# A hybrid decoder trunk in float32 parts: low parts of projection weights by adding transfers, and convolution taps spread over the mixer stage

## The chip, the core and the metric

The kernel runs on one core of a Trainium2 chip. The core has TensorE (matmuls; PE in the profile), VectorE (DVE), ScalarE (ACT), GpSimd (POOL) and SyncE (SP), each with its own queue of instructions that it works through in order, and 16 DMA engines that they share. The metric is the time of one execution on the device in microseconds, as a median of several runs.

## The reference, cut to what matters

Two layers over a sequence of 1024 tokens with 1024 features, in float32. Each layer is a mixer and then a convolutional feed-forward network, both between two RMS norms. The mixer's input projection has 24 blocks of 128 columns, which feed four groups:

```python
proj = rms_norm(x, norm_mix_pre[l]) @ w_in[l]
(c_a, c_gate, sb_q, sb_k, sb_v, r_q, r_k, r_v, r_g, sc_b, sc_c, sc_h) = jnp.split(proj, 12, axis=-1)
y_conf = conformer_conv(c_a, c_gate, conf_dw_w[l], conf_dw_b[l], conf_ln_g[l], conf_ln_b[l])
y_sb = merge_heads(stick_breaking_attention(split_heads(sb_q), split_heads(sb_k), split_heads(sb_v)))
y_ret = retention_mixer(r_q, r_k, r_v, r_g, ret_norm_g[l])
y_sc = short_gated_conv(sc_b, sc_c, sc_h, sc_conv_w[l])
mix = jnp.concatenate([y_conf, y_sb, y_ret, y_sc], axis=-1) @ w_out[l]
...
def conformer_conv(a, gate, dw_w, dw_b, ln_g, ln_b):
    h = a * jax.nn.sigmoid(gate)
    h = causal_dwconv(h, dw_w) + dw_b     # 31 taps
    return jax.nn.silu(layer_norm(h, ln_g, ln_b))
```

Stick-breaking attention takes scores, a running sum along the keys of their softplus, an exponential, and a product with the values. Retention works in chunks of 128 tokens with a state carried from chunk to chunk.

## The kernel before, in words

**Number format.** A float32 matmul is made of three in a faster rounded format: every operand is split into a rounded high part and the rest, the low part, and high x high, high x low and low x high are added up in PSUM. For a block of projection weights (`load_weight`, lines 189 to 196) a transfer brings the 512 KB into `wr`, of which there is one buffer; ScalarE rounds it into `wh` (L193), and VectorE subtracts to get `wl` (L195). `wh` and `wl` have two buffers each, so the split of a block waits until the projection before the current one is done with its buffers.

**Slots.** The mixer's work is interleaved by hand. The 24 projections run in `IN_ORDER`; each has eight steps of six matmuls (L210), and after each step `run_slot` runs whatever has been entered for that slot: a slot is one such step, and 192 of them make the projections of a layer. The first two projections go together (`project_pair`, slots 0 to 15); projection n covers slots 8n to 8n + 7. What a projection gives is taken from PSUM by `evict`, and that enters later work: ten units of stick-breaking per pair of heads, scores at `SB_SLOT` + 6 k (L361 to L381: matmuls, three ScalarE passes, a VectorE step L375, scans on VectorE L379, an exponential), their transposes seven slots later and their products with the values ten slots later; retention from `RET_SLOT` on (state steps L474 to L479, scores L494 to L497, output L513 to L523, each output taken from PSUM by one ScalarE and two VectorE steps); the conformer's layer norm at `LN_SLOT`. The region's TensorE instructions keep the order in which they are traced. The order of the other engines is made by a scheduler from its own estimates of time and from priorities.

**The long convolution.** When the sigmoid gate of a conformer pair is done (kind "cg"), the convolution is entered in `conv`: a start on ScalarE (L268) and 30 taps on VectorE (L261), two times a layer. `run_slot` adds 0.8 to a credit in each slot, from the first slot on, and traces one step of the convolution for each whole credit, with a priority 1000 lower than other work.

**PSUM.** Projections alternate between banks 0 and 1. Stick-breaking's scores use bank 2, and retention takes bank 2 or the free one of the other two, by the slot (`bank`): bank 2 if the slot's number modulo 8 is not 0, 2 or 4.

**Tables.** ScalarE's sigmoid needs another function table than its exponential and logarithm; `ln_exp_tables` asks for the latter back.

Of the kernel before, what the change touches and what calls it, by code (L numbers as in the profile page):

```python
# [7 lines left out]
F32 = mybir.dt.float32  # L8
F32R = mybir.dt.float32r
AF = mybir.ActivationFunctionType  # L10
ALU = mybir.AluOpType
# [24 lines left out]


IN_ORDER = [
# [7 lines left out]
]  # L46
CONV_LATER = 1000
CONV_RATE = ((999, 0.8),)
REGION = 2
SB_SLOT = (20, 108)  # L50
SB_STEP = (6.0, 5.5)
SB_T = 7
SB_V = 10
RET_SLOT = 94, 160
RET_AT = (0, 6, 9, 12, 14, 17, 18, 23, 25), (0, 7, 9, 12, 14, 17, 18, 24, 26)
RET_PRE = 6, 3
LN_SLOT = 170
HOLD = 30
ROT_HOLD = 0
CONVH = 0  # L60
# [7 lines left out]
OTHER = (0, 2, 4)  # L68
HPR = 1000
HPW = 0  # L70
WPOOL = []
UPOOL = ()
SKEW = 0
NPLAIN = 3
# [12 lines left out]
def trunk_kernel(ctx, tc, x, w_in, w_out, w_up, w_down, params, gains, consts, rope, out):  # L87
    nc = tc.nc
# [25 lines left out]
    def ualloc(dt=F32, shape=(P, T)):  # L114
        s = free.pop(0)
        count[0] += 1
        t = big.tile(list(shape), dt, tag=f"u{s}", name=f"u{s}_{count[0]}")
        slot_of[id(t)] = (s, t)
        return t

    def ufree(*ts):
        for t in ts:
            free.append(slot_of.pop(id(t))[0])
# [15 lines left out]
    def ln_exp_tables():  # L139
        tc.keep_in_program_order(nc.scalar.preload_act_table_set("natural_log_exp_and_others"))  # L140
# [48 lines left out]
    def load_weight(src, eng):  # L189
        raw = wp.tile([P, KT, P], F32, tag="wr", name="wr", bufs=WR)  # L190
        nc.sync.dma_start(raw, src)
        wh = wp.tile([P, KT, P], F32R, tag="wh", name="wh")
        nc.scalar.copy(wh, raw)  # L193
        wl = wp.tile([P, KT, P], F32R, tag="wl", name="wl")
        eng.tensor_sub(wl, raw, wh.bitcast(F32))  # L195
        return wh, wl

    queue = []
# [351 lines left out]

    psum("pp")
    nc.scalar.preload_act_table_set("natural_log_exp_and_others")
    queue += [(w_in[0, n], nc.gpsimd if n in WPOOL else nc.vector) for n in range(24)]
    hhs = []
    for t in range(NB + SKEW):
        if t == XP:
# [22 lines left out]
    for l in range(DEPTH):  # L579
# [5 lines left out]
        def at(slot, fn, order=0):  # L585
            events.setdefault(slot, []).append((order, fn))

        conv = []
        credit = [0]
        slot = [0]  # L590

        def bank():

            s = slot[0]
            return (s // 8 + 1) % 2 if s < 192 and s % 8 in OTHER else 2

        def run_slot():
            for _, fn in sorted(events.pop(slot[0], ()), key=lambda e: e[0]):
                fn()
            credit[0] += next(r for end, r in CONV_RATE if slot[0] < end)  # L600
            while conv and credit[0] >= 1:
                credit[0] -= 1
                with tc.high_priority(offset=-CONV_LATER):
                    if next(conv[0], 0) == 0:
                        conv.pop(0)
            slot[0] += 1

        wo = []
# [15 lines left out]
        def evict(kind, i, ps, cs):  # L624
            if kind == "ca":
                st["a", i] = ualloc()
                nc.scalar.copy(st["a", i], ps)
            elif kind == "cg":
                s = ualloc()
                nc.scalar.activation(s, ps, AF.Sigmoid)  # L630
                if i == 1:
                    ln_exp_tables()
                nc.vector.tensor_mul(s, s, st["a", i])
                ufree(st["a", i])
                conv.append(conv_start(L, s, i, y, lambda h: at(slot[0] + HOLD, lambda: ufree(h))))
            elif kind == "sq":
                st["q"] = stick_q(ps)
                st["units"] = []
                for k in range(10):
                    u = dict(q=st["q"][k // 5], k=st["k"][k // 5], hh=k // 5, grp=SB_GROUPS[k % 5],  # L640
                             last=k % 5 == 4)
                    st["units"].append(u)
                    base = SB_SLOT[i] + int(SB_STEP[i] * k)
                    at(base, lambda u=u: stick_scores(u))
                    at(base + SB_T, lambda u=u: stick_transpose(u))
                    at(base + SB_V, lambda u=u: stick_values(u))
            elif kind == "sk":
                st["k"] = stick_k(ps)
            elif kind == "sv":
                ve = ualloc()  # L650
                nc.scalar.copy(ve, ps)
                v2 = []
                at(slot[0] + 2, lambda: v2.extend(value_tiles(ve)))
                y[2 + i] = ualloc()
                for u in st["units"]:
                    u.update(v=v2, y=y[2 + i])
            elif kind == "rk":
                st["rk"] = rotate(ps, cs, later)
            elif kind == "rq":
                st["rq"] = rotate(ps, cs, later)  # L660
            elif kind == "rv":
                rv = ualloc()
                nc.scalar.copy(rv, ps)
                k, kt2, q2, v2, gate = [], [], [], [], []
                rk, rq = st["rk"], st["rq"]
                st["gate"] = gate

                def keys():
                    h, lo = ualloc(F32R), ualloc(F32R)
                    split(h, lo, rk)  # L670
                    k.extend((h, lo))
                    kt2.extend(key_tiles(rk))

                def queries():
                    v2.extend(value_tiles(rv))
                    for half in range(2):
                        q2.append(ualloc(F32R, (P, 4, 2, P)))
                        split(q2[half][:, :, 0, :], q2[half][:, :, 1, :],
                              rq[:, half * 512:(half + 1) * 512].rearrange("p (c t) -> p c t", t=P))
                    ufree(rq)  # L680

                at(RET_SLOT[i] - RET_PRE[0], keys)
                at(RET_SLOT[i] - RET_PRE[1], queries)
                ret = retention(L, i, q2, k, kt2, v2, gate, y, bank)
                def ret_step(ret=ret):
                    with tc.high_priority(offset=HPR):
                        next(ret)

                for a in RET_AT[i]:
                    at(RET_SLOT[i] + a, ret_step)  # L690
            elif kind == "rg":
                gs = ualloc()
                nc.scalar.activation(gs, ps, AF.Silu)
                ln_exp_tables()
                st["gate"].append(gs)
            elif kind == "xh":
                st["h"] = ualloc()
                nc.scalar.copy(st["h"], ps)
            elif kind == "xc":
                nc.vector.tensor_mul(st["h"], st["h"], ps)  # L700
                acc = ualloc()
                w = L + C_SW + 3 * i
                nc.scalar.activation(acc, st["h"], AF.Copy, scale=par[:, w + 2:w + 3])
                for _ in conv_taps(acc, st["h"], w, 3):
                    pass
                ufree(st["h"])
                y[6 + i] = acc
            elif kind == "xb":
                nc.vector.tensor_mul(y[6 + i], y[6 + i], ps)

        sq = []
        at(LN_SLOT, lambda: layer_mean(y, sq))
        at(LN_SLOT + LN_VAR, lambda: layer_var(L, y, sq))
        cs = None
# [328 lines left out]
        with tc.manual_schedule(engines={mybir.EngineType.PE}):  # L1043
# [4 lines left out]
            for j in range(NPLAIN, NF):  # L1048
                end = j == NF - 1
# [14 lines left out]
        for ci, ch in enumerate(chunks):  # L1064
            final = ci == len(chunks) - 1
            if final:
                if not last:
                    queue += [(w_in[l + 1, n], nc.gpsimd if n in WPOOL else nc.vector) for n in range(24)]
                    prefetch(2)
                g_post, g_pre = gain(4 * l + 3), None if last else gain(4 * l + 4)  # L1070
            pairs = [loads[j] for j in ch]
            gs, ws = [p[0] for p in pairs], [p[1] for p in pairs]
            for t in range(NB):
                if final and last and t == NB - 1:
                    down_end(gs, ws, t)
                else:
                    down_tok(gs, ws, t, ci == 0, final)
                if t in (0, 1) and ci and todo and not final:
                    j, where = todo.pop(0)
                    loads[j] = down_load(j, where)  # L1080
            if places[ci] is None:
                for g, w in zip(gs, ws):
                    ufree(*g, *w)
            if ci == 0:
                for _ in range(4):
                    j, where = todo.pop(0)
                    loads[j] = down_load(j, where)
# [74 lines left out]
```

## Time and profile before

| | |
|---|---|
| median of three runs | 2382.75 us (2381.59 to 2386.46) |
| the profiled execution | 2386.67 us, of which 2384.9 is the span from the first to the last instruction |
| TensorE busy | 2297.3 us (96% of the span), 10596 matmuls; granted clock 0.986 |
| VectorE busy | 1674.2 us (70%) |
| ScalarE busy | 1080.7 us (45%) |
| GpSimd busy | 196.5 us (8%) |

Busy time of TensorE is the time in which at least one matmul is under way; the matmuls overlap, 390 ns each at a spacing of 228 ns. The granted clock is the share of full speed that the chip allowed TensorE. The mixer of layer 0 lies from about 20 to 580 us of the span, that of layer 1 from about 1210 to 1770, each with the output projection and the beginning of the feed-forward network behind it; the rest is the feed-forward network.

### The profile page before, as it was taken

The numbers are of one execution on the slowest core, as the hardware profiler recorded it, in microseconds if no ns is written. First come the engines' busy times: TensorE is split into PE (matmuls) and PEld (weight loads), VectorE is DVE, ScalarE is ACT, GpSimd is POOL, SyncE is SP. The second block draws the span as 40 slices with busy tenths as digits, with TensorE's granted clock in tenths as the row PEclk, the third lists the DMA queues.
The fourth block names the chain that finished last, engine by engine and source line by source line (L and its number), as shares of the span: only waits on it lengthen the run. The fifth ranks groups of instructions, "written<-read, shape, count | busy, mean of one in ns | idle before, by whom it ended". The sixth has DMA issues, their size and how long they took to land.

```text
span 2384.9 us, 26334 instructions
## 1 busy us (share of the span) xinstructions
PE 2297.3 (96%) x10596; PEld 1885.0 (79%) x10596; DVE 1674.2 (70%) x1749; ACT 1080.7 (45%) x1463; POOL 196.5 (8%) x84
## 2 busy tenths in 40 slices
PE   7998999999999999999999989999999999999998
PEld 6876787787888888788778767877888888888886
DVE  4699877559777777644556998775598777774445
ACT  5663565434455445421246535654344554453112
POOL 0000000000000000643210000000000000016420
PEclk9998999999999999999999989999999999999999
DMA  4212212412122224522222122123122222235223
GB/s 150 71 53 63 62 36 88 138 48 92 68 88 89 80 80 143 183 80 98 80 80 71 53 62 62 36 95 135 53 89 80 80 80 89 87 121 176 84 71 124
DMA packets 58810, 209.87 MB, mean 88 GB/s; under 512 B 7104, under 2 KB 7872, under 8 KB 58688
## 3 DMA queue, kind: packets, MB, share of 16 engines
q1 hardware_dynamic: 58688, 208.19, 26.7%
q8 instruction: 83, 1.36, 0.2%
q14 instruction: 39, 0.32, 0.0%
HBM read 159.93 MB, written 39.85 MB: 84 GB/s over the span
## 4 chain that ended last, share of the span: by engine, by line
PE 38%; DVE 7%; ACT 3%; DMA 1%; issue 1%; DVEq 0%; SPq 0%
PE pp L984 10%; PE pp L210 9%; PE ppx L901 8%; PE ppy L901 4%; DVE u L261 2%; PE ppz L901 2%; PE pp L738 1%; DVE u L182 1%; ACT u L151 1%; DMA wr<-in_w_out 1%; PE op L409 1%; DVE u L379 1%; DVE u L167 1%; PE tp L396 0%; DMA wr<-in_w_up 0%
## 5 line engine op out<-in xcount | busy, mean ns | idle before, releaser
L261 DVE SCALAR_TENSOR_TENSOR u<-u,par,u 128x1023 f32<-128x1023 f32 (+10 forms) x280 | 356.3, 1284 | 28.6 <-ACT u L793 24.4
L210 PE MATMUL pp<-hH,wh 128*128 128x512 f32 x960 | 327.2, 411 | 1.0 <-DVE u L182 0.5
L997 DVE TENSOR_TENSOR u<-u,pp 128x1024 f32<-128x1024 f32 x143 | 174.6, 1221 | 209.9 <-PE pp L984 209.8
L210 PE MATMUL pp<-hL,wh 128*128 128x512 f32 x960 | 312.7, 396 | 0.0
L210 PE MATMUL pp<-hH,wl 128*128 128x512 f32 x960 | 311.5, 395 | 0.0
L984 PE MATMUL pp<-u,u 128*128 128x512 f32 x1152 | 266.0, 392 | 6.1 <-ACT u L955 4.6
L984 PEld LDWEIGHTS pp<-u,u 128*128 128x128 f32 x1152 | 216.6, 189 | 52.4 <-ACT u L955 5.4
L974 POOL TENSOR_TENSOR hH<-u,hH 128x1024 fp32r<-128x1024 f32 x24 | 58.1, 2451 | 1946.5 <-ACT hH L973 1946.5
L210 PEld LDWEIGHTS pp<-hL,wh 128*128 128x128 f32 x960 | 183.6, 191 | 40.4
L210 PEld LDWEIGHTS pp<-hH,wl 128*128 128x128 f32 x960 | 183.2, 191 | 40.3
L210 PEld LDWEIGHTS pp<-hH,wh 128*128 128x128 f32 x960 | 172.6, 193 | 37.5 <-issue 5.9
L738 PE MATMUL pp<-u,hH 128*128 128x512 f32 x512 | 140.2, 392 | 0.4 <-ACT u L181 0.4
L984 PE MATMUL pp<-hH 128*128 128x512 f32 x576 | 131.5, 389 | 0.0
L984 PEld LDWEIGHTS pp<-hH 128*128 128x128 f32 x576 | 108.1, 188 | 22.4
L901 PE MATMUL ppx<-u,wh 128*128 128x512 f32 x384 | 118.4, 389 | 0.3 <-ACT u L926 0.3
L793 ACT ACTIVATE u<-u,par 128x1024 f32<-128x1024 f32 x76 | 87.8, 1156 | 67.4 <-DVE u L947 65.6
L738 PEld LDWEIGHTS pp<-u,hH 128*128 128x128 f32 x512 | 95.0, 188 | 20.4 <-ACT u L181 1.2
L195 DVE TENSOR_TENSOR wl<-wr,wh 128x1024 fp32r<-128x1024 f32 x60 | 73.3, 1221 | 50.9 <-ACT wh L193 50.7
L973 ACT CAST u<-u 128x1024 fp32r<-128x1024 f32 x48 | 50.2, 1052 | 128.9 <-DMA u<-in_w_down 85.7
L901 PE MATMUL ppx<-u,hH 128*128 128x512 f32 x352 | 108.4, 389 | 0.0
L193 ACT CAST wh<-wr 128x1024 fp32r<-128x1024 f32 x60 | 63.0, 1051 | 71.3 <-PE pp L210 57.1
L379 DVE TENSOR_TENSOR_SCAN u<-pp,u 128x1023 f32<-128x1023 f32 (+3 forms) x64 | 87.8, 1403 | 0.7
(240 smaller groups left out, 4400.3 us busy)
## 6 DMA issues: line engine op xcount, KB each, us to landing
wr<-in_w_up SPq DMA_DIRECT2D x50, 512.0 KB, 3.5
wr<-in_w_in SPq DMA_DIRECT2D x48, 512.0 KB, 3.5
gd<-u SPq DMA_DIRECT2D x44, 512.0 KB, 2.9
u<-in_w_down SPq DMA_DIRECT2D x44, 512.0 KB, 4.3
u<-gd SPq DMA_DIRECT2D x44, 512.0 KB, 3.9
u<-in_w_up SPq DMA_DIRECT2D x38, 512.0 KB, 4.3
xs<-u SPq DMA_DIRECT2D x24, 512.0 KB, 2.6
u<-xs SPq DMA_DIRECT2D x24, 512.0 KB, 3.4
```

The costliest lines, as they stand in the source:

```text
L193: nc.scalar.copy(wh, raw)
L195: eng.tensor_sub(wl, raw, wh.bitcast(F32))
L210: nc.tensor.matmul(ps[:, half * 512:(half + 1) * 512], w[:, kt, :], m[:, 4 * half:4 * half + 4, kt, :], start=(kt == 0 and m is hH and w i ...
L261: eng.scalar_tensor_tensor(acc[:, lo:hi], src[:, lo - s:hi - s], wc, acc[:, lo:hi], ALU.mult, ALU.add)
L379: nc.vector.tensor_tensor_scan(rev, z[:, o + 1:e + 1][:, ::-1], rev, r[:, e:e + 1], ALU.add, ALU.add)
L738: nc.tensor.matmul(ps[:, hs], a[:, t, k, :], w[:, hs], start=(k == 0 and a is hH and w is wo[k][0]), stop=(k == KT - 1 and a is hL))
L793: nc.scalar.activation(acc, ps, AF.Copy, scale=par[:, w + 2:w + 3])
L901: nc.tensor.matmul(ps, a[:, kt, :], x(m, kt), start=start and kt == 0 and a is wh and m == 0, stop=kt == 3 and a is wl, skip_group_check=True)
L973: nc.scalar.copy(h, raw)
L974: (nc.gpsimd if len(loads) >= 4 else nc.vector).tensor_sub(lo, raw, h.bitcast(F32))
L984: nc.tensor.matmul(ps[:, hs], a[:, ts_], w[:, hs], start=(i == 0 and w is h and a is gh), stop=(i == len(gs) - 1 and a is gl))
L997: nc.vector.tensor_add(facc[t], facc[t], ps)
```

## The change

Four things change together.

- The first conformer pair is projected first: columns "ca" 0 and "cg" 0 are the pair of slots 0 to 15, and stick-breaking's first keys, queries and values follow in slots 16 to 39. Its units start at slot 36 instead of 20. The exponential's tables are asked for after each of the two gates, which are no longer next to each other. The layer norm moves from slot 170 to 176.
- The steps of the convolution get 0.75 credit a slot up to slot 36 and 0.42 after; credit is held at 2 at most, and is 0 while no convolution is entered.
- Each tap is queued on VectorE behind the last instruction other than a tap that had been traced for VectorE three slots back (`CONV_LAG`). This is an order within VectorE's queue, not a wait for another engine.
- For projections from the third on (22 of 24 in a layer) the low part is made without VectorE: ScalarE writes the raw weights times -1 in the rounded format into `wl`, and a transfer issued by GpSimd adds the raw weights from HBM to it.

```diff
 IN_ORDER = [
-    ("sk", 0, 6), ("sq", 0, 4), ("sv", 0, 8),
-    ("ca", 0, 0), ("ca", 1, 1), ("cg", 0, 2), ("cg", 1, 3),
+    ("ca", 0, 0), ("cg", 0, 2), ("sk", 0, 6), ("sq", 0, 4), ("sv", 0, 8),
+    ("ca", 1, 1), ("cg", 1, 3),
...
-CONV_RATE = ((999, 0.8),)
+CONV_RATE = ((36, 0.75), (999, 0.42))
+CONV_LAG = 3
-SB_SLOT = (20, 108)
+SB_SLOT = (36, 108)
-LN_SLOT = 170
+LN_SLOT = 176
...
-        eng.tensor_sub(wl, raw, wh.bitcast(F32))
+        if eng is not None:
+            eng.tensor_sub(wl, raw, wh.bitcast(F32))
+            return wh, wl
+
+        nc.scalar.activation(wl, raw, AF.Copy, scale=-1.0)
+        nc.gpsimd.dma_start(wl, src, accum_op=ALU.add)
         return wh, wl
...
-    queue += [(w_in[0, n], nc.gpsimd if n in WPOOL else nc.vector) for n in range(24)]
+    queue += [(w_in[0, n], None if n >= 2 else nc.vector) for n in range(24)]
...
+        seen = [None]
+        marks = []
+
+        def mark_slot():
+
+            traced = nc.cur_bb.bb.instructions
+            mark = marks[-1] if marks else None
+            for i in reversed(traced):
+                if i is seen[0]:
+                    break
+                if i.engine == mybir.EngineType.DVE and i.name not in taps:
+                    mark = i
+                    break
+            seen[0] = traced[-1]
+            marks.append(mark)
+
+        taps = set()
+
         def run_slot():
             for _, fn in sorted(events.pop(slot[0], ()), key=lambda e: e[0]):
                 fn()
-            credit[0] += next(r for end, r in CONV_RATE if slot[0] < end)
+            mark_slot()
+            credit[0] = min(credit[0] + next(r for end, r in CONV_RATE if slot[0] < end), 2) if conv else 0
             while conv and credit[0] >= 1:
                 credit[0] -= 1
-                with tc.high_priority(offset=-CONV_LATER):
+                mark = marks[max(0, len(marks) - 1 - CONV_LAG)]
+                with ExitStack() as late:
+                    late.enter_context(tc.high_priority(offset=-CONV_LATER))
+                    if mark is not None:
+                        late.enter_context(tc.issue_after(mark))
+                    traced = nc.cur_bb.bb.instructions
+                    n = len(traced)
                     if next(conv[0], 0) == 0:
                         conv.pop(0)
+                    taps.update(i.name for i in traced[n:])
             slot[0] += 1
...
             elif kind == "cg":
                 s = ualloc()
                 nc.scalar.activation(s, ps, AF.Sigmoid)
-                if i == 1:
-                    ln_exp_tables()
+                ln_exp_tables()
```

The same choice of `None` for blocks from the third on stands where layer 1's weights are entered.

## Rows read from the trace of the kernel before

**Rows 1.** Busy time by stretch (us); x counts instructions, PEclk is the granted clock.

```profile
48.00:420.00 372.00, 351.02 (x1761) 285.52 (x1760) 298.53 (x349) 210.40 (x270) 0.00 (x0) 0.97 0.22 66
60.00:120.00 60.00, 60.00 (x312) 50.79 (x311) 39.76 (x44) 39.34 (x50) 0.00 (x0) 1.00 0.22 71
120.00:280.00 160.00, 139.94 (x687) 113.03 (x687) 152.49 (x171) 77.24 (x101) 0.00 (x0) 0.94 0.21 60
1300.00:1460.00 160.00, 141.56 (x677) 114.07 (x676) 151.86 (x167) 76.87 (x99) 0.00 (x0) 0.91 0.20 57
```

The columns of these rows: the stretch, its length, then busy us and instructions of PE, PEld, DVE, ACT and POOL, the granted clock, the DMA engines' busy share, GB/s.

**Rows 2.** The same view in slices of 20 us, layer 0.

```profile
160.00:180.00 20.00, 18.40 (x94) 15.33 (x93) 19.75 (x23) 8.26 (x14) 0.00 (x0) 1.00 0.16 53
180.00:200.00 20.00, 19.12 (x103) 15.96 (x102) 19.87 (x22) 6.91 (x8) 0.00 (x0) 1.00 0.09 27
...
220.00:240.00 20.00, 13.25 (x44) 9.96 (x43) 19.05 (x20) 4.92 (x7) 0.00 (x0) 0.74 0.22 77
240.00:260.00 20.00, 15.71 (x69) 12.67 (x68) 16.78 (x16) 8.78 (x12) 0.00 (x0) 0.83 0.26 79
...
280.00:300.00 20.00, 20.00 (x105) 16.74 (x104) 16.84 (x20) 12.35 (x17) 0.00 (x0) 1.00 0.19 53
...
340.00:360.00 20.00, 19.89 (x117) 16.96 (x116) 18.08 (x29) 10.79 (x19) 0.00 (x0) 1.00 0.07 27
```

**Rows 3.** The same view of line L210 alone: PE, PEld, clock, DMA.

```profile
48.00:120.00 72.00, 59.74 (x246) 44.58 (x245) 1.00 0.26 83
120.00:280.00 160.00, 104.39 (x406) 77.23 (x405) 0.94 0.21 60
```

**Rows 4.** VectorE's groups by line, 120 to 280 us.

```profile
L261 DVE SCALAR_TENSOR_TENSOR u<-u,par,u 128x1019 f32<-128x1019 f32 (+29 forms) x56 | 69.2, 1263 | 0.5
L379 DVE TENSOR_TENSOR_SCAN u<-pp,u 128x1023 f32<-128x1023 f32 (+7 forms) x13 | 18.2, 1433 | 0.1
L182 DVE TENSOR_TENSOR u<-tp,u 128x512 fp32r<-128x512 f32 x19 | 12.3, 683 | 0.0
L195 DVE TENSOR_TENSOR wl<-wr,wh 128x1024 fp32r<-128x1024 f32 x9 | 11.0, 1220 | 2.0 <-ACT wh L193 2.0
L375 DVE SCALAR_TENSOR_TENSOR u<-pp,u 128x1024 f32<-128x1024 f32 (+1 forms) x7 | 8.0, 1141 | 1.1 <-ACT u L373 1.1
```

The columns: line, engine, operation, tiles and shapes, count | busy us, mean ns of one | idle us before, and what ended it.

**Rows 5.** Timeline of VectorE: start us, us, instruction, count.

```profile
231.15 0.69 DVE L522 TENSOR_TENSOR u<-pp,u 64x512 f32<-64x512 f32 x1
231.77 1.25 DVE L261 SCALAR_TENSOR_TENSOR u<-u,par,u 128x1007 f32<-128x1007 f32 x1
233.05 0.68 DVE L523 TENSOR_TENSOR u<-pp,u 64x512 f32<-64x512 f32 x1
```

**Rows 6.** TensorE's waits, whole span: us in total, times, longest.

```profile
PE pp L513 <- DVE u L379: 8.6, 2, 4.3
...
PE pp L361 <- DVE u L379: 7.3, 6, 1.7
```

**Rows 7.** ScalarE's groups by line, 20 to 420 us.

```profile
L193 ACT CAST wh<-wr 128x1024 fp32r<-128x1024 f32 x23 | 24.2, 1051 | 22.7 <-PE pp L210 21.3 <-DMA wr<-in_w_in 1.4
...
L630 ACT ACT_TABLE_LOAD x2 | 2.6, 1283 | 0.0
```

**Rows 8.** Timeline of ScalarE at the end of the first pair, layer 0.

```profile
42.90 1.06 ACT L193 CAST wh<-wr 128x1024 fp32r<-128x1024 f32 x1 [9.12 <-PE pp L210]
...
48.57 1.02 ACT L328 ACTIVATE u<-pp 64x1024 fp32r<-64x1024 f32 x1 [1.18 <-PE pp L210]
```

**Rows 9.** The chain that ended last, in order of time: start us, us, what.

```profile
1222.60 9.13 PE pp L210 x40
```

**Rows 10.** DMA issues of the page: KB each, median us to landing.

```profile
wr<-in_w_in SPq DMA_DIRECT2D x48, 512.0 KB, 3.5
gd<-u SPq DMA_DIRECT2D x44, 512.0 KB, 2.9
...
u<-gd SPq DMA_DIRECT2D x44, 512.0 KB, 3.9
```

More of the change, by code (lines that the diff above doesn't have):

```diff
@@ L70 @@
 HPW = 0
-WPOOL = []
 UPOOL = ()
@@ L1067, in trunk_kernel @@
                 if not last:
-                    queue += [(w_in[l + 1, n], nc.gpsimd if n in WPOOL else nc.vector) for n in range(24)]
+                    queue += [(w_in[l + 1, n], None if n >= 2 else nc.vector) for n in range(24)]
                     prefetch(2)
```

## The prediction

> **What bounds the kernel now.** I read the page's busy times first (the table above): TensorE is busy 96% of the span, so only time in which TensorE waits, or runs at its lower clock, can be won back. Then the windows of the two mixer stages [rows 1]. From 60 to 120 us TensorE is busy all the time, with VectorE at 40 of 60 us. From 120 to 280 us in layer 0, and from 1300 to 1460 us in layer 1, VectorE is at 152 of 160 us, and TensorE is idle 20.1 and 18.4 us. The granted clock falls there to 0.94 and 0.91 (a mix of the levels 2.4 and 1.2 GHz): busy time times the missing share is 8.4 and 12.7 us. Together that is 59.6 us. A second reading counts matmuls: 312 in 60 undisturbed us make 5.2 per us, so the 687 and 677 matmuls need 132.1 and 130.2 us, and 28 and 30 us of each 160 are lost. The two readings agree: **58 us** are there to be won. In slices of 20 us [rows 2] the reader sees how it is lost. With VectorE full and the clock still at 1.00 TensorE loses 1.6 and 0.9 us a slice; at 220 to 260 us it loses 6.8 and 4.3 us and the clock falls to 0.74 and 0.83. With VectorE at 16.8 or 18.1 of 20 us, and hardly a tap, it loses 0.0 and 0.1 us.
>
> What fills VectorE there? Grouped by line, 56 taps of the long convolution (L261) take 69.2 us of the 160 [rows 4]. The timeline of VectorE [rows 5] shows the harm: between each two steps of retention's output (L522, L523) stands one or a pair of taps, so a chain that TensorE waits for gets 1.25 us longer at every link. TensorE's waits name L379, the scan of stick-breaking, whose score bank the next matmuls want [rows 6].
>
> **The change part by part.**
>
> *Taps.* Before, credit grows by 0.8 a slot from the first slot on, with no convolution yet there to use it, so more than thirty taps are traced at once at slot 47, with the lowest priority, and the rest soon after. Slots are counted in groups of six matmuls of L210: 246 of them stand from 48 to 120 us and 406 from 120 to 280 [rows 3], which is slots 16 to 56 and 56 to 123. After, the first convolution starts at slot 15: 21 slots at 0.75 give 15 steps, then 0.42 a slot, and the 64 steps end near slot 151. In slots 56 to 123 that leaves 68 x 0.42 = 28.6 taps for 56: 27.4 fewer, at 69.2 / 56 = 1.24 us each, makes -34 us of VectorE.
>
> *Low parts.* For 22 projections of a layer VectorE's subtraction (1.22 us, L195) becomes a second ScalarE pass (as L193, 1.05 us) [rows 4, 7] and an adding transfer from GpSimd's queue. In the same slots 9 x 1.22 = -11 us. ScalarE gains 22 x 1.05 = 23 us, and two table loads of 1.28 us a layer for the sigmoid that now stands alone [rows 7]: 26 us more on 210 of 372 us [rows 1]; it is covered. If ScalarE lacked the room, the 26 us would fall on the stick-breaking chain, which is a rival below.
>
> *Stick-breaking 16 slots later.* The first ten units move from slots 20 to 74 to slots 36 to 90, the second ten stay. Slots 56 to 123 then hold nine scored units instead of seven. One costs VectorE 1.14 (L375) + 18.2 / 7 = 2.6 (L379) + about two splits of 0.68 [rows 4], with the small additions of L417 and L418 some 6 us by my estimate: +12 us.
>
> So VectorE's load there goes from 152 to 152 - 34 - 11 + 12 = 119 us. TensorE's own work there is 160 - 29 = 131 us and some 8 us more for the two units (my estimate from 12 us between units less projections). 119 of 139 is 86%, inside the slices of [rows 2] that lose 0.0 to 0.1 us. But taps still stand in the queue, so I take a quarter of the mean of 1.6 and 0.9 us: 0.3 to 0.4 us a slice over slots 16 to 151, some 257 us (72 for slots 16 to 56, 131 to 123, and 28 more at the same 1.9 us): **5 us a layer**. The bounds are 1 us (the loaded slices without taps) and 16 us (the full ones).
>
> *The first late transfer.* The weight after the first pair cannot be split before the pair's first half ends: its copy starts at 42.90 us, and the pair ends at 48.57 [rows 8]. TensorE reads a low part after four matmuls, 4 x 9.13 / 40 = 0.9 us later [rows 9], so at 49.5. The new chain: two ScalarE passes, to 45.0 us, then the adding transfer. The trace has none. From below it is a plain load of the same 512 KB, 3.5 us; from above load, store and load again, 3.5 + 2.9 + 3.9 = 10.3 us [rows 10]. That is a stall of 0 to 5.8 us. I take one read of the weight and one pass over the destination, 3.5 + 2.9 = 6.4 us, since an addition must read both: landing at 51.4, **1.9 us a layer**. The Trainium skill, DMA: Bandwidth & Descriptors, section Anatomy of one DMA, gives 2.0 us plus bytes over 436 GB/s for a transfer of GpSimd's, an estimate of 3.2 us without the addition; by it this term would be 0, and the sum 3.8 us better for two layers. No run here shows it yet.
>
> *The later transfers.* The buffers of the projection before come free when a projection starts, and the next needs its low part 48 x 0.228 + 0.9 = 11.8 us later if nothing stands between its matmuls, and 257 / 17 + 0.9 = 16.0 us later on average over those 17 projections. The chain is 2.1 + 6.4 = 8.5 us: hidden. At 10.3 us it is 12.4, and the few bare projections lose 0.6 us each. Behind the waiting transfer on GpSimd's queue stands only the next one: GpSimd is idle in the stage [rows 1]. On SP's queue the next load waits for the raw weight's buffer, and the rotary copies and key copies queue behind it; that buffer is now free after ScalarE's second pass instead of after VectorE's subtraction, so they can only come sooner. The transfers add 44 reads of 512 KB to engines that are busy 0.22 of the stage.
>
> *A new wait.* The last unit of the first stick-breaking, scored at slot 90, uses the score bank that retention's first matmuls want at slot 94. The same pair three slots apart costs 4.3 us before (L513 waiting for L379) [rows 6]; four slots apart gives one slot, 6 x 0.228 = 1.4 us, more, and VectorE is less full. Bounds 0 and 4.3; I take **1.5 us a layer**.
>
> *The layer norm six slots later* (176, its second part 181) still ends ahead of the output projection at slot 192, with some 11 slots in hand: nothing.
>
> **Sum.** 58 us, less 2 x (5 + 1.9 + 1.5) = 17, makes 41 won. The profiled execution took 2386.7 us (span 2384.9 and 1.8 around it): 2345.7. It stood 3.9 us above the median of the three runs, so against the median I say **2342 us**.
>
> **The rivals.**
>
> *TensorE goes on waiting for the chains.* The taps are not the only length in a chain: ScalarE's passes and the scans stay, and the convolution now also runs in slots 120 to 151, where VectorE had room. For it: L361's waits for L379 are 1.7 us at the longest, about one tap [rows 6], so waits of that size survive wherever one tap is left. Against it: the loaded slices without loss. If the loss falls to 16 us a layer, the full slices' rate, the gain is 58 - 2 x (16 + 3) = 20 us: 2363.
>
> *The adding transfers arrive late (slower).* If a transfer takes D us, a projection waits when 2.1 + D passes 16.0 us on average; the 41 us are eaten when 44 transfers are each 0.9 us late, which is D of about 14.8, more than four plain loads. At D of 17 us the loss is 44 x 3.1 = 136 us: near 2478. A way to it: GpSimd makes the transfer's descriptors itself, and VectorE's instructions, back to back in this stage, keep it from doing so. The Trainium skill, SBUF — State Buffer, section Who interferes with whom, says that VectorE blocks GpSimd's descriptor writing in its two-port modes, and that tensor_tensor has none; the VectorE groups here are tensor_tensor, scans and scalar_tensor_tensor, so by it the blocking should not come, and no run here shows it. Against the rival: 10.3 us is already the sum of three plain transfers.
>
> *The stall only moves.* TensorE's order is fixed by hand; what is not lost to retention's chain is lost to the score bank at slot 94 at 4.3 us and to ScalarE's 26 us more a layer, where stick-breaking and the lone sigmoid meet. Then 2380, no difference.
>
> **How the numbers follow.** Forecast 0.63 (its own range 2324 to 2355), chains still waiting 0.18, late transfers 0.12, moved stall 0.07. By the count of matmuls at the best rate shown without loss that has the same mix, 105 in 20 us [rows 2], 58 us hold; with nothing left over the time would be 2325, and the idle time also hides restarts that the rows don't show, so the range begins at 2318. It ends at 2376, above the second case; beyond it lie the late transfers and the moved stall. A change under 0.2%, 4.8 us, can't be told from none here. Faster: 0.63 + 0.18 = 0.81; same 0.07; slower 0.12.
>
> **What would show it.** In the changed kernel's profile VectorE should be near 86% in slots 56 to 123, in place of 95%, and the granted clock should stay near 1.00 where it was 0.74. No subtraction L195 for projections after the second; GpSimd's transfers land 5 to 8 us after they are issued. TensorE should wait some 2 us for the low part at the first projection after the pair, and nowhere else for a low part. L513's wait for L379 should stand near the first retention step. I would be wrong if TensorE waits for low parts throughout (late transfers), or if VectorE is relieved and TensorE idles as before.

## The result, and the profile after

The changed kernel is slower: 2402.49 us median of four runs (2398.64 to 2405.79) against 2384.61 for the kernel before, a ratio of 1.0075 with a 95% interval of 1.0054 to 1.0097. 41 us were to be won and 18 were lost. The profiled execution took 2398.64 us, its span is 2396.9, 12.0 longer than before: the execution profiled before was the longest of its kernel's runs, this one is the shortest of its own. In what follows ratios are always to runs of the kernel before on the same chip; 1% is 24 us. Line numbers behind `load_weight` are 5 higher than before, behind `run_slot` 30 higher.

Busy time by stretch, three of the stretches of [rows 1]:

```profile
48.00:420.00 372.00, 350.48 (x1758) 285.24 (x1757) 273.09 (x325) 226.47 (x289) 18.17 (x21) 0.97 0.40 94
...
120.00:280.00 160.00, 143.53 (x728) 117.29 (x727) 118.60 (x146) 94.21 (x125) 7.79 (x9) 0.95 0.39 89
1300.00:1460.00 160.00, 143.96 (x738) 118.26 (x737) 119.29 (x146) 94.20 (x125) 7.76 (x9) 0.96 0.39 92
```

VectorE's load from 120 to 280 us fell from 152.5 to 118.6 us; I had worked out 119. And yet TensorE is busy 143.5 us there, little more than the 139.9 before, with the granted clock at 0.95. VectorE is no longer full, and TensorE still waits: it idles 16.5 of the 160 us, nearly as much as before (20.1), which is one of the two signs that the prediction named for being wrong. The slices of the same view (as [rows 2], and two of the output projection) show where:

```profile
160.00:180.00 20.00, 20.00 (x108) 16.88 (x107) 17.29 (x20) 15.91 (x21) 0.86 (x1) 1.00 0.25 53
180.00:200.00 20.00, 13.14 (x63) 10.69 (x62) 12.07 (x17) 11.32 (x17) 0.86 (x1) 0.83 0.24 53
220.00:240.00 20.00, 17.09 (x94) 13.07 (x92) 14.57 (x16) 10.04 (x13) 0.86 (x1) 1.00 0.40 105
240.00:260.00 20.00, 17.23 (x70) 14.29 (x71) 11.38 (x13) 9.59 (x13) 0.86 (x1) 0.74 0.39 106
...
420.00:440.00 20.00, 16.19 (x68) 11.93 (x66) 10.60 (x10) 4.55 (x5) 0.00 (x0) 1.00 0.41 131
440.00:460.00 20.00, 18.00 (x67) 14.66 (x68) 5.74 (x5) 4.02 (x4) 0.00 (x0) 0.83 0.27 79
```

The slices that [rows 2] show at 160 and 220 us are better, 20.0 for 18.4 and 17.1 for 13.3 us. The one at 180 us is bad now, 13.1 for 19.1 us, with VectorE at 12 of 20. And two slices of the output projection hold 68 and 67 matmuls where there were 87 and 84 (TensorE was busy 19.8 and 18.1 us there before, at a clock of 1.00).

Counted by TensorE's instructions in the two traces (six matmuls of L215, before L210, are a slot), the 24 projections of a layer take 396.4 and 396.7 us (layers 0 and 1) in place of 396.6 and 399.8, and the output projection behind them 105.6 and 103.7 in place of 97.4 and 95.9. Inside the projections something was won and lost again: in layer 0, slots 104 to 112 take 22.7 us for 32.6, and slots 88 to 96 take 28.2 for 16.3. TensorE's waits over the whole span (us in total, times, longest) put names to them:

```profile
PE tp L455 <- DVE u L182: 12.9, 4, 5.8
PE pp L768 <- ACT u L181: 10.3, 6, 3.7
PE pp L366 <- DVE u L384: 8.4, 4, 2.4
PE pp L215 <- DMA wl<-in_w_in: 6.4, 3, 3.5
...
PE pp L518 <- DVE u L384: 5.7, 2, 2.9
```

L518's wait for L384, which is L513 and L379 in [rows 6], fell from 8.6 to 5.7 us; all waits of retention's output (L518) together fell from 21.0 to 11.3. The first, second and fourth rows stand for what was added: retention's key transposes (L455) waited 1.1 us before, the output projection (L768) 0.4, and the low part of the first projection after a pair not at all. The third (L366, stick-breaking's scores) stood at 7.3 before.

**The first place, slot 88.** TensorE, ScalarE and VectorE, by their timelines (start us, us, instruction, idle before and what ended it):

```profile
179.62 1.11 PE L414 MATMUL op<-u,u 128*128 128x256 f32 x8
180.57 0.60 PE L455 MATMUL tp<-ident,u 128*128 128x128 f32 x4
187.00 1.11 PE L455 MATMUL tp<-ident,u 128*128 128x128 f32 x4 [5.83 <-DVE u L182]
```

```profile
179.08 1.28 ACT L723 ACT_TABLE_LOAD   x1
180.37 1.02 ACT L723 ACTIVATE u<-pp 128x1024 f32<-128x1024 f32 x1
181.41 1.28 ACT L140 ACT_TABLE_LOAD   x1
183.22 1.06 ACT L386 ACTIVATE u<-u 128x1024 f32<-128x1024 f32 x1 [0.52 <-DVE u L384]
184.18 1.04 ACT L199 ACTIVATE wl<-wr 128x1024 fp32r<-128x1024 f32 x1
185.25 0.36 ACT L421 COPY u<-op 64x256 f32<-64x256 f32 x1
185.64 0.59 ACT L181 CAST u<-tp 128x512 fp32r<-128x512 f32 x1
```

```profile
186.25 0.69 DVE L182 TENSOR_TENSOR u<-tp,u 128x512 fp32r<-128x512 f32 x1 [0.18 <-ACT u L181]
186.98 0.42 DVE L423 TENSOR_TENSOR u<-op,u 64x256 f32<-64x256 f32 x1
```

The product with the values (L414), the key transposes and the layer norm share two PSUM tiles. At slot 88 the values of stick-breaking's eighth unit (slot 36 + 42 + 10) take one and the first four transposes the other. The next four start when the first four have been split into high and low part (L181, then L182), so they wait for that tile; the values' tile is read until later still (L423). L181 stands in ScalarE's queue behind the retention gate with its two table loads, an exponential, the new second pass (L199) and the values' own readout (L421). The first four transposes are done at 181.2 us, and L181 starts 4.5 us after. Before, the last values of these units stood at slot 84.

**The second place, the output weights.** They too come through the one raw buffer, block by block. ScalarE's timeline, and SyncE's, which issues the loads, with VectorE's half of the split between them:

```profile
404.85 2.37 ACT L306 ACTIVATE u<-u,par 128x1024 f32<-128x1024 f32 x2
...
414.78 2.93 ACT L181 CAST hH<-u 128x1024 fp32r<-128x1024 f32 x3
417.61 1.05 ACT L181 CAST u<-wr 128x1024 fp32r<-128x1024 f32 x1
418.56 3.90 ACT L181 CAST hH<-u 128x1024 fp32r<-128x1024 f32 x4
427.90 1.05 ACT L181 CAST u<-wr 128x1024 fp32r<-128x1024 f32 x1 [5.44 <-DMA wr<-in_w_out]
```

```profile
422.39 1.22 DVE L182 TENSOR_TENSOR u<-wr,u 128x1024 fp32r<-128x1024 f32 x1
```

```profile
402.95 0.33 SPq L644 DMA_DIRECT2D wr<-in_w_out  x1
415.63 7.20 SPq L249 DMA_DIRECT2D u<-in_x  x2
423.63 0.33 SPq L644 DMA_DIRECT2D wr<-in_w_out  x1
```

ScalarE does not split the block issued at 402.95 before 417.61, since the layer norm's passes (the last is L306) and the splits of the mixed heads (L181 into hH) stand ahead of it. VectorE follows at 422.39, behind its own half of those splits, and only then is the buffer free. So the next load starts 20.7 us after this one, and TensorE waits for the last blocks one by one.

**The third place, the first low part** after the pair of layer 0:

```profile
42.62 1.05 ACT L193 CAST wh<-wr 128x1024 fp32r<-128x1024 f32 x1 [9.12 <-PE pp L215]
43.57 1.06 ACT L199 ACTIVATE wl<-wr 128x1024 fp32r<-128x1024 f32 x1
```

```profile
48.54 0.61 PE L215 MATMUL pp<-hL,wh 128*128 128x512 f32 x2
51.58 0.87 PE L215 MATMUL pp<-hH,wl 128*128 128x512 f32 x2 [2.43 <-DMA wl<-in_w_in]
52.25 1.05 PE L215 MATMUL pp<-hH,wh 128*128 128x512 f32 x2
```

```profile
wl<-in_w_in POOLq DMA_DIRECT2D x44, 512.0 KB, 7.4
```

The wait is 2.4 us here and 3.5 in layer 1; behind it pairs of matmuls take 1.05 us instead of 0.61, at the lower clock; the last row is the page's DMA issue, the median from issue to landing in us.

### The profile page after: what moved, and what is told of

Its sections match the earlier page's. It is cut to its first block, busy times and chain, and to the rows that moved or that the text cites. A ratio compares the mean times of both kernels' runs of the same rounds, so it can differ in the third digit from the quotient of the medians.

```text
span 2396.9 us, 26404 instructions
## 1 busy us (share of the span) xinstructions
PE 2297.6 (96%) x10596; PEld 1883.5 (79%) x10596; DVE 1626.8 (68%) x1705; ACT 1114.0 (46%) x1505; POOL 234.7 (10%) x128
## 3 DMA queue, kind: packets, MB, share of 16 engines
q8 instruction: 83, 1.36, 0.2%
## 4 chain that ended last, share of the span: by engine, by line
PE 35%; DVE 7%; ACT 5%; DMA 2%; issue 1%; DVEq 0%; SPq 0%; ACTq 0%
PE pp L1014 10%; PE ppx L931 8%; PE pp L215 6%; PE ppy L931 4%; PE pp L768 2%; PE ppz L931 2%; DVE u L266 1%; DVE u L384 1%; DVE u L182 1%; DMA wr<-in_w_out 1%; DMA wl<-in_w_in 1%; ACT u L181 1%; DVE u L380 1%; ACT u L377 0%; ACT u L151 0%
## 5 line engine op out<-in xcount | busy, mean ns | idle before, releaser
L266 DVE SCALAR_TENSOR_TENSOR u<-u,par,u 128x1023 f32<-128x1023 f32 (+6 forms) x280 | 359.1, 1283 | 40.8 <-ACT u L823 24.4
L215 PE MATMUL pp<-hH,wh 128*128 128x512 f32 x960 | 325.7, 410 | 0.4 <-ACT hH L181 0.4
L215 PE MATMUL pp<-hH,wl 128*128 128x512 f32 x960 | 311.7, 395 | 6.4 <-DMA wl<-in_w_in 6.4
L215 PE MATMUL pp<-hL,wh 128*128 128x512 f32 x960 | 312.0, 396 | 0.0
L215 PEld LDWEIGHTS pp<-hH,wl 128*128 128x128 f32 x960 | 182.6, 191 | 47.8 <-DMA wl<-in_w_in 8.1
L215 PEld LDWEIGHTS pp<-hL,wh 128*128 128x128 f32 x960 | 183.0, 191 | 40.2
L215 PEld LDWEIGHTS pp<-hH,wh 128*128 128x128 f32 x960 | 172.6, 192 | 36.3 <-issue 5.5
L1004 POOL TENSOR_TENSOR hH<-u,hH 128x1024 fp32r<-128x1024 f32 x24 | 58.2, 2452 | 1208.6 <-ACT hH L1003 1208.6
L768 PE MATMUL pp<-u,hH 128*128 128x512 f32 x512 | 145.6, 402 | 10.8 <-ACT u L181 10.3
L768 PEld LDWEIGHTS pp<-u,hH 128*128 128x128 f32 x512 | 96.9, 192 | 34.4 <-ACT u L181 12.8
L200 POOL DMA_DIRECT2D wl<-in_w_in x44 | 38.2, 868 | 710.9 <-ACT wl L199 588.3
L182 DVE TENSOR_TENSOR u<-tp,u 128x512 fp32r<-128x512 f32 x96 | 62.8, 685 | 44.1 <-ACT u L181 43.8
```

The lines of the kernel that those rows point to most:

```text
L182: nc.vector.tensor_sub(l, src, h.bitcast(F32))
L200: nc.gpsimd.dma_start(wl, src, accum_op=ALU.add)
L215: nc.tensor.matmul(ps[:, half * 512:(half + 1) * 512], w[:, kt, :], m[:, 4 * half:4 * half + 4, kt, :], start=(kt == 0 and m is hH and w i ...
L266: eng.scalar_tensor_tensor(acc[:, lo:hi], src[:, lo - s:hi - s], wc, acc[:, lo:hi], ALU.mult, ALU.add)
L768: nc.tensor.matmul(ps[:, hs], a[:, t, k, :], w[:, hs], start=(k == 0 and a is hH and w is wo[k][0]), stop=(k == KT - 1 and a is hL))
L1004: (nc.gpsimd if len(loads) >= 4 else nc.vector).tensor_sub(lo, raw, h.bitcast(F32))
```

## The experiments

The first four were to tell two theories apart: that the stalls had only moved (A), or that the adding transfers cost the time (B). "The mended kernel" is that of the fifth experiment.

**Low parts on VectorE again.**

```diff
-    queue += [(w_in[0, n], None if n >= 2 else nc.vector) for n in range(24)]
+    queue += [(w_in[0, n], nc.vector) for n in range(24)]
```

The same is done for layer 1.

> The changed kernel with the low parts of all 24 projections made by VectorE's subtraction again; order of projections, taps and slots stay as changed. Theory A (the stalls moved: stick-breaking's tail meets retention's start near slot 88, and the later layer norm delays the output weights): the wait for the first adding transfer goes, 4 us a layer, and VectorE gets 27 us a layer more work, so 2390 to 2410 us against 2402, and the 5.8 us wait of the key transposes (L455) and the waits of the output projection for ScalarE stay. Theory B (the adding transfers are what costs, by ScalarE's second pass and by traffic): the loss goes, 2375 to 2386 us, and those two waits go too.

Measured 0.9985 (0.9973 to 0.9998): 0.9%, 21 us, are back. On the time B is right and A wrong. On the places it is the other way round for one of the two: the key transposes wait nearly as long as in the changed kernel (5.4 us at the longest for 5.8), and the output projection waits a third as long.

```profile
PE tp L455 <- DVE u L182: 10.8, 2, 5.4
...
PE pp L768 <- ACT u L181: 3.5, 3, 2.3
```

**Layer norm at slot 170.**

```diff
-LN_SLOT = 176
+LN_SLOT = 170
```

> The changed kernel with the layer norm at slot 170 as before. Theory A: the split of the fourth block of output weights no longer stands behind the layer norm on ScalarE; the output projection's waits for ScalarE (10.3 us in the span, 7 to 8 us a layer with the slower clock behind them) go, and the time falls by 12 to 15 us, to 2387 to 2391. Theory B: the output weights are late because of ScalarE's extra passes and of the transfers, not the norm's slot; within 4 us of 2402.

Measured 1.0018 (1.0005 to 1.0030), 14 us back; L768 waits 0.2 us in the span instead of 10.3. As A said.

**Stick-breaking's first units closer.**

```diff
-SB_STEP = (6.0, 5.5)
+SB_STEP = (5.5, 5.5)
```

> The changed kernel with stick-breaking's first ten units 5.5 slots apart instead of 6, so that its last values come at slot 95 instead of 100 and none stand at slot 88, where retention's keys are transposed. Theory A: the excess of the projection at slots 88 to 95, 10 us a layer, falls to 4 or less, and the time by 8 to 14 us, to 2388 to 2394. Theory B: no collision at that slot, so the wait only moves to another place; within 4 us of 2402.

Measured 1.0019 (1.0007 to 1.0031), 13 us back; L455's wait falls from 12.9 to 3.0 us. As A said. The edit moves nine of the ten units, though, so it is not shown that all of the 13 us are this one meeting's.

**The adding transfers alone, on the kernel before.** The edit is that of `load_weight` and of the two `queue` lines.

> The kernel before with the adding transfers alone; order, taps and slots as before. Theory A: two costs of about 2 to 4 us for the first transfer of a layer, and 11 us less VectorE work a layer in the stretch where VectorE is full, which TensorE gets back at half to full rate: 2365 to 2382 us against 2385. Theory B: 2395 to 2405, with TensorE waiting for low parts or for what ScalarE does late.

Measured 1.0083 (1.0066 to 1.0099), 20 us lost: B again, and against my sum, by which VectorE's relief should have paid for the first transfers. TensorE waits for two low parts, 8.5 us in all, and slots 16 to 24, where they fall, take 19.3 and 18.8 us in this trace for 12.1 before: some 14 of the 20 us. So neither theory was enough. Theory C took both: the taps win, and three costs eat it.

**Three undone together.** Low parts on VectorE, norm at 170, step 5.5.

> The changed kernel with three things undone or mended together: low parts by VectorE, layer norm at slot 170, stick-breaking's first units 5.5 slots apart. Theory C, formed after the first four runs: the spread taps do win some 18 us a layer, and three separate costs eat it, each with its place: the adding transfers (first projection after the pair, output weights), stick-breaking's tail against retention's start, the late norm. Then the three add up but for what two of them share in the output projection (7 us): 2402 - 21 - 15 - 15 + 7 = 2358, between 2352 and 2366. Rival D: the three are one shortage seen at three places, and mending one mends most: 2372 to 2384.

Measured 0.9916 (0.9902 to 0.9930), 2364.16 us: **20 us faster than the kernel before**, and 38 us faster than the changed one. Singly the three gave back 0.90, 0.57 and 0.56%, 2.03% or 48 us; 10 of those are shared, 3 more than the 7 I took for the output projection. C holds; the rival D (one shortage at three places) would have been at 2372 or more.

**Low parts on GpSimd.**

```diff
-    queue += [(w_in[0, n], None if n >= 2 else nc.vector) for n in range(24)]
+    queue += [(w_in[0, n], nc.gpsimd if n >= 2 else nc.vector) for n in range(24)]
```

> The changed kernel with the low parts of the third and later projections subtracted by GpSimd (2.4 us as its other subtractions take) in place of ScalarE's second pass and the adding transfer; VectorE is as free as with the change. Theory C: the loss of the transfers goes, since the chain to the first low part is 1.05 + 2.4 us instead of 2.1 + 7, and ScalarE has 23 us a layer less: 2378 to 2388. Rival: GpSimd's reads and VectorE's hold each other up, VectorE's taps get longer than 1.27 us, and it stays above 2392.

Measured 1.0032 (1.0020 to 1.0045), 2390 us, between the two expectations: 10 of the 21 us come back. The rival's mechanism is there; how much of the other 11 us it makes is not shown. Of VectorE's groups, 120 to 280 us, this is the first:

```profile
L266 DVE SCALAR_TENSOR_TENSOR u<-u,par,u 128x1000 f32<-128x1000 f32 (+24 forms) x25 | 34.0, 1360 | 0.3
```

With the low parts on VectorE 25 taps take 31.6 us, 1264 ns each. The median is 1.27 us in both, so a few taps are held up: the longest takes 2.8 us in this stretch (3.3 between 48 and 420 us), against 1.28.

**The third projection's low part on VectorE too.** `None if n >= 3`.

> The changed kernel with the third projection's low part also by VectorE, so that the first adding transfer of a layer is that of the fourth. Theory C: the wait at the first projection after the pair (excess 4.3 and 3.8 us) goes, the rest of the transfers' cost, in the output projection, stays: 2392 to 2396. Rival: the wait moves to the next projection, which has no other TensorE work between its steps either: 2398 to 2403.

Measured 1.0063 (1.0048 to 1.0079): 3 us back, which the intervals do not tell from none, 2399 us, as the rival said. TensorE's wait for low parts is 6.4 us in all as in the changed kernel, in three waits: in layer 0 it moved to the next projection. Starting the transfers one weight later does not help.

**The taps alone, on the kernel before.** Old order and slots, low parts on VectorE, 0.55 credit a slot, held at 2, queued three slots back.

```diff
-CONV_RATE = ((999, 0.8),)
+CONV_RATE = ((999, 0.55),)
+CONV_LAG = 3
```

> The kernel before with nothing changed but the taps: 0.55 credit a slot (the 64 steps end near slot 163), credit held at 2, queued three slots back; old order, old slots, low parts by VectorE. If spreading the taps is what wins: the excess of 17 us a layer at slots 104 to 111 falls below 9, and the time to 2350 to 2368. If the earlier start is needed, since the taps now fill slots 120 to 163 as well: 2376 or more.

Measured 0.9950 (0.9934 to 0.9966), 2371 us, between the two expectations: 12 us won by the taps alone, without the earlier start.

**The same slots and credit without the queueing.** The mended kernel of the fifth experiment.

```diff
-                    if mark is not None:
-                        late.enter_context(tc.issue_after(mark))
```

> The mended kernel (low parts by VectorE, norm at 170, step 5.5; 2364 us) with the taps at the same slots and the same credit, but not queued behind VectorE's work of three slots back. If the spread credit alone wins: 2360 to 2368. If the queueing does part of it, taps go ahead of chain steps again and the excess of slots 88 to 119 grows: 2372 or more.

Measured 1.0000 (0.9989 to 1.0010): the queueing is worth 0.84%, 20 us, all that the mended kernel had won over the kernel before. Taps in the stretch of slots 88 to 103 (stretch, length, VectorE's busy us and count, clock, DMA), first without and then with the queueing:

```profile
184.00:223.00 39.00, 20.14 (x17) 0.96 0.21 55
```

```profile
177.00:211.00 34.00, 8.22 (x7) 1.00 0.25 63
```

Traced at the same pace, seventeen taps stand there again instead of seven. The list of credits alone does not spread them; my reading, which no run shows, is that the scheduler sets low-priority work wherever it believes VectorE to be idle. All engines from 120 to 280 us, in the same order:

```profile
120.00:280.00 160.00, 143.39 (x725) 116.81 (x724) 132.52 (x158) 84.83 (x113) 0.00 (x0) 0.95 0.21 62
120.00:280.00 160.00, 149.07 (x767) 121.47 (x767) 136.13 (x164) 90.18 (x122) 0.00 (x0) 0.97 0.22 61
```

Without the queueing VectorE is 20 us less busy there than in the kernel before (152.5), and the time is the same. So its load is not what sets the time.

**The adding transfers on the mended kernel.** Norm at 170 and step 5.5 only.

> The mended kernel with the adding transfers back for 22 of 24 projections of a layer. Theory C: what is left of their cost with the norm early is the wait at the first projections of a layer, 4 to 8 us a layer with the clock behind it, against 27 us a layer less VectorE work that now hides under TensorE: 2370 to 2382. If VectorE is what still paces the stage: 2364 or below.

Measured 0.9957 (0.9943 to 0.9970), 2371.6 us, 0.41% or 10 us more than with VectorE's subtraction. VectorE is at 122 us of 160 instead of 136 (120 to 280 us), and the relief does not pay for what the transfers and the second pass cost. Were VectorE the pace of the stage, it should have.

**ScalarE's second pass without the transfer.** Low parts on VectorE, the negated copy kept ahead of the subtraction.

```diff
+            if twice:
+                nc.scalar.activation(wl, raw, AF.Copy, scale=-1.0)
             eng.tensor_sub(wl, raw, wh.bitcast(F32))
```

Here `twice` is set for the projections from the third on.

> The changed kernel with low parts by VectorE (2381.6 us) and ScalarE's second pass kept for the 22 projections (written into the low part's buffer and then overwritten by VectorE's subtraction, which waits for it), without any transfer. If the second pass makes the cost of the adding transfers: 2392 to 2402. If the transfer itself makes it: 2381 to 2387.

Measured 1.0046 (1.0029 to 1.0063): 0.61% or 15 us above the first experiment's kernel, which has no second pass. So some 15 of the 21 us (7 to 21 by the two intervals) are the pass itself, with VectorE's subtraction waiting for it. The rest may be the transfer: slots 16 to 24 take 10.9 us in this trace as in the first experiment's, and 15.2 and 14.7 in the changed kernel's. The waits, with line numbers 2 higher than in the changed kernel, are those of the change:

```profile
PE tp L457 <- DVE u L182: 14.3, 4, 6.5
PE pp L770 <- ACT u L181: 10.9, 6, 4.0
```

**Two of retention's steps later**, on the mended kernel.

```diff
-RET_AT = (0, 6, 9, 12, 14, 17, 18, 23, 25), (0, 7, 9, 12, 14, 17, 18, 24, 26)
+RET_AT = (0, 6, 9, 12, 14, 18, 20, 23, 25), (0, 7, 9, 12, 14, 17, 18, 24, 26)
```

> The mended kernel with retention's last two output steps of the first pair one and two slots later (112 and 114 for 111 and 112), so that none uses the score bank that the second stick-breaking's first unit, scored at slot 108, still holds. Theory C (what is left of the stage's loss is such meetings of hand-made slots, not VectorE's load): L518's wait for L384 (2.9 us a layer) and the slower clock behind it go, 2350 to 2360. If VectorE's load is what is left: 2361 to 2368.

Measured 0.9856 (0.9839 to 0.9873), **2349 us: 35 us faster than the kernel before**, 52 than the changed one. That is 1 us below the first expectation's range. L518's wait for L384 is gone; it was 5.7 us of idle time in the span, and 14 us came back. VectorE is busier than in the mended kernel (whose row stands at the ninth experiment), and so is TensorE:

```profile
120.00:280.00 160.00, 151.67 (x787) 123.53 (x786) 140.21 (x168) 92.63 (x125) 0.00 (x0) 0.98 0.23 65
1300.00:1460.00 160.00, 152.93 (x803) 125.04 (x802) 141.82 (x169) 91.36 (x123) 0.00 (x0) 0.99 0.23 63
```

With VectorE at 140 of 160 us TensorE works through 787 matmuls in the stretch where the changed kernel, with VectorE at 119, gets through 728.

## Why the prediction was wrong

*VectorE's load* came out as worked out, 119 us forecast and 118.6 measured, in part by luck: the taps fell by 37.6 us for 34 (25 stand in the stretch for 28.6), and the other work grew by 14.7 us for 12. The error behind the sum was that TensorE gets back what VectorE gives up: 58 us were put down to VectorE's load, and the load is not what sets TensorE's time. The ninth experiment has 20 us less of it there than the kernel before and the same time; the twelfth has 22 us more than the change and is 52 us faster. TensorE waits for single instructions, and what stands ahead of those decides.

*The taps* were right in direction: what helped is where they stand. The step did not see that the queueing is what does it: without it the mended kernel's credits, order and slots together are worth nothing (ninth experiment).

*ScalarE's 26 us more, "it is covered"*: this step failed. The share of the stage (226 of 372 us) says nothing about one pass in the wrong place. Some 15 us hang on the second pass (eleventh experiment): with it the output projection waits 10.9 us for ScalarE's splits, without it 3.5, and in the traces it takes 105.7 and 103.4 us for 100.8 and 97.6. At the key transposes the pass adds little; slots 88 to 96 take 28.0 and 29.1 us with it, 28.1 and 27.7 without. I had named the case as a rival (the stall only moves) and given it 0.07 together with another; the time is worse than that rival's 2380.

*The adding transfer* was sized about right: 7.4 us at the median for my 6.4, within 3.5 to 10.3. The first one's term was too small: its stall is 2.4 and 3.5 us for 1.9, and with the lower clock behind it slots 16 to 24 are 4.3 and 3.8 us longer than without transfers (first experiment). The later ones are hidden but for 0.5 us in layer 1. The rival of late transfers throughout is refuted. The estimate of 3.2 us from the Trainium skill (DMA: Bandwidth & Descriptors, Anatomy of one DMA), for a transfer that does not add, is under half of it. The Trainium skill (SBUF — State Buffer, Who interferes with whom) gives tensor_tensor no two-port mode that would block GpSimd's descriptor writing; of scans and scalar_tensor_tensor, which the prediction counted in, that section says nothing. The trace agrees, and shows no block by the other two forms either: the 44 issues take GpSimd 0.86 to 1.01 us each, and the nine between 120 and 280 us, where VectorE is at 118.6 of 160, have landed after 6.0 to 7.9.

*The new wait at slot 94, 1.5 us a layer,* did not come; the meeting was six slots earlier and at other tiles, and moving it away gives 13 us (third experiment). I had looked at the score bank and not at the pair of tiles that transposes, values and norms share. The wait for the score bank that the prediction had read in the kernel before, three slots apart at 4.3 us, it took only as a measure; it stayed at 2.9 us a layer, and undoing it is what the twelfth experiment does.

*The layer norm six slots later, "nothing"*: this step failed too. I counted eleven slots of room for the norm itself, and not who stands behind it on ScalarE: the output weights' splits, whose one buffer makes each late split a late load. It is 14 us with the second pass there (second experiment). How much the later norm costs without that pass was not timed alone; in the first experiment, which has the one without the other, the output projection waits 3.5 us instead of 10.3 and takes 5 us more over both layers than in the kernel before, an estimate from its trace.

*The sum.* The spread taps and the new order are worth 20 us net of their other effects (fifth experiment), the three costs 38. That is the 18 lost. The nearest that any run came to the 41 us is 35 (twelfth experiment).

## What to carry to other kernels

A full engine in a stage with a stalled TensorE does not show that its load is the cause: name the instruction that TensorE waits for, and ask who stands ahead of it on its engine. When work is moved in a hand-made order, list for every slot which buffers, PSUM tiles too, are held by what is now in flight there, and what queues behind each pass that is added, even on an engine that is half idle. Low-priority filler needs a place in the queue: at the same pace, queued behind the chain it was worth 20 us here, and left to the scheduler's gaps nothing.

## What the runs showed of the hardware that was not expected

An adding transfer of 512 KB from HBM into SBUF took 5.9 to 9.4 us from issue to landing, 7.4 at the median, where a plain load of the same bytes took 3.5 before. With these transfers beside it the plain load of the projection weights went to 3.9 us at the median.

VectorE's taps were held up when GpSimd subtracted in SBUF: a tap of 1.26 us took 1.36 on average from 120 to 280 us, and up to 2.8 us, with GpSimd subtractions of 2.5 us in the stretch (sixth experiment). That GpSimd was held up in turn is not shown; its other subtractions (L1004) take 2.4 to 2.5 us. The Trainium skill, SBUF — State Buffer, section Who interferes with whom, says that a VectorE instruction with two inputs in SBUF contends with a GpSimd instruction that reads SBUF; the trace agrees.

A stall costs more than its idle time. Taking away 5.7 us of TensorE's idle waits gave 14 us (twelfth experiment; in the two traces the projections are 9.8 us shorter). From 220 to 240 us, the slice with that wait, the mended kernel's granted clock is 0.76, a mix of the levels 2.4 and 1.2 GHz, with 63 matmuls; without the wait it is 0.86, with 86.
